# Keys of both inputs from one moving operand, and six modulation pieces one block earlier

## The chip, the cores and the metric

One core of one Trainium2 chip runs the whole kernel. The metric is the device time of one execution in microseconds. Its engines are named as in the profile: PE multiplies matrices, and PEld is its loading of weights (the stationary operand); DVE, ACT and POOL work on vectors; SP issues most transfers. One matmul step `X @ W` of this kernel keeps fp32 precision by splitting both operands into a high and a low part (`hi`, `lo`) and adding hi x hi, hi x lo and lo x hi.

## The reference, cut to what matters

x and ctx are 256 x 2048 each; the width of the attention is 1024 (16 heads of 64).

```python
hl = modulate(rms_norm(xl, norm1_g), mod_l[0], mod_l[1])      # x,   256 x 2048
hc = modulate(rms_norm(xc, norm1_g), mod_c[0], mod_c[1])      # ctx, 256 x 2048
zl = hl @ w_in + b_in                                         # conv | gMLP | q | k | v | gates
zkv = hc @ w_in[:, K_OFF:G_OFF] + b_in[K_OFF:G_OFF]           # ctx: keys and values alone
y_na = neighbourhood_attention(q, k, v, kc, vc, rpb)          # x attends to itself and to ctx
y = g_conv * conv_branch(zl) + g_sgu * sgu_branch(zl) + g_att * (y_na @ w_na_out)
xl = xl + mod_l[2] * (y @ w_o + b_o)
h2 = modulate(rms_norm(xl, norm2_g), mod_l[3], mod_l[4])
xl = xl + mod_l[5] * (square(relu(h2 @ w_ff1 + b_ff1)) @ w_ff2 + b_ff2)
out = rms_norm(xl, final_g)
```

The modulation vectors `mod_l`, `mod_c` are `silu(c) @ w_mod` for the two condition vectors.

## The kernel before, in words

All large weights come through one stream (`Stream`, L69). SP loads pieces of 512 KB into one of 8 `raw` buffers (L96); for a weight that is multiplied, ACT copies the high part (`whi`, L102) and DVE subtracts to get the low part (`wlo`, L105), each with 4 buffers. A list of steps is written by hand: each step names its pieces and a function that issues its work, and pieces are fetched up to 4 ahead (AHEAD).

*Stage 1, keys and values.* The 16 blocks of 128 along the width (`kt`) come in five blocks (BLOCKS, L34: 2, 2, 4, 4 and 4 of them). Each begins when its part of the first modulation is there (`mod_block`): `rows` (L393) transposes the normed inputs, and ACT and DVE write the scaled input and its low part into `hl` (high part in the first 256 of 512 columns, low part in the second). A heap unit of 4 KB a partition holds two kt of one input (L400 to L404). Then `kv_block` (L416) does the keys: `kfn` goes over tiles of 128 key columns (index i, nt) and both inputs v, with a PSUM bank for each (four banks `acc` in all). `mm_w` issues for each kt one matmul of 512 columns (`whi` by high and low part, L203) into the whole bank, then one of 256 (`wlo` by the high part, L205) into its second half. The two halves must be joined: ACT copies the second half (L438), DVE adds the first (L439), and POOL adds it to the keys so far, `kT` (L440); in block 0 ACT adds the bias (L435) and DVE joins (L436). Values (`vfn`, `mm_x`, L212 to L215) take the input as the stationary operand and the weights as the moving one, three matmuls of 512 columns per kt, and DVE adds the bank to `vN` (L456).

*Modulation pieces.* The other four modulation chunks are made by DVE alone: each piece (`mod_cols`, L932) brings two 128x512 row blocks of `w_mod` by SP, and DVE does two multiply-adds into `ga` (L944, L946). Every eighth piece ends with PE work (`col_finish`, transposes L975, or `row_finish`). `mod_steps(n)` puts n of them into the list; after each step of the last key and value block (bi 4) there are MODS_KV = 2, so 12 in all (L1026 to L1030).

*Stage 2* makes queries (`q_done`), convolution inputs (`a1_done`, `a2_done`, into `uT`), the gMLP halves (`gu`, `sv`), with the attention's steps between: `att_keys` (L538) writes the split keys into new units `kh`, `kl` and loads a bias tile (`bias_tile`, L563), `att_scores`, `att_transpose` and `att_out` follow, the last into `oT`. The 248 taps of the convolution are DVE instructions (`conv_taps`, L682 to L692), put between steps and reaching into stage 3; with the last tap `uT` goes out of use.

*Stage 3, the branches* (L1094 on), n = 0 attention, n = 1 gMLP, n = 2 convolution: for each of four column blocks cb, the gate's matmuls with x (`g_done`, L893, then a tanh) and the branch's output projection (`y_done`, L901), which for n = 0 writes into a new unit `mN[cb]`. Beside n = 0 the gMLP's norm and mixing run (`sgu_var`, L848: squares into a unit `svq`; `sgu_norm`, L861; `sgu_mix`, L865). All units come from one pool of HEAP = 27 (L57, `unit`, L183); a new one waits until the earlier user of its place is done.

Of the kernel before, what the change touches and what calls it, by code (L numbers as in the profile page):

```python
# [8 lines left out]
F32 = mybir.dt.float32  # L9
# [6 lines left out]
P = 128  # L16
# [15 lines left out]
GC1 = 0.7978845608028654  # L32

BLOCKS = [(0, 2), (2, 2), (4, 4), (8, 4), (12, 4)]  # L34
MODS_KV = 2
EARLY = 4
EARLY0 = 3
EARLYX = 2
# [125 lines left out]
def tile_block(ctx: ExitStack, tc: tile.TileContext, x, c, ctxt, c_ctx, w_mod, b_mod, norm1_g, norm2_g,  # L164
# [138 lines left out]

    m1A = cp.tile([P, NK, 2], F32, name="m1A")
    m1B = cp.tile([P, NK, 2], F32, name="m1B")
    hl = [[None] * NK, [None] * NK]
    kT = [None] * 8
    vN = [None] * 4

# [33 lines left out]
    def mod_block(bi):  # L343
        k0, nk = BLOCKS[bi]
        cols = nk * P
        rt = 1024 // cols
        gb = {}

        def mk(j, r0):
            def fn(raw):  # L350
                if r0 == 0:
                    gb[j] = aux("gemv")
                for r in range(rt):
                    g = r0 + r
                    q = g % 4
                    PE.matmul(gb[j][32 * q : 32 * q + 32, :cols], lhsT=cst[:, g], rhs=raw[:, r],
                              start=g < 4, stop=g >= NK - 4, tile_position=(0, 32 * q))
                if bi == 0 and (j, r0) != (1, NK - rt):
                    for r in range(rt):
                        q = (r0 + r) % 4  # L360
                        PE.matmul(warm()[32 * q : 32 * q + 32, :cols], lhsT=cst[:, r0 + r], rhs=raw[:, r],
                                  start=True, stop=True, tile_position=(0, 32 * q))
            return fn

        steps = []
        for j in range(2):
            for r0 in range(0, NK, rt):
                steps.append(([piece(w_mod, r0, rt, j * D + k0 * P, cols, False)], mk(j, r0)))

        def post(vs=(0, 1)):  # L370
            if vs[0] == 0:
                vectors()
            rows(vs)
            if bi == 0 and vs == (0,):
                for i in range(12):
                    PE.transpose(warm()[:, :P], gb["ge"][:, :P], ident)

        def vectors():
            gv = tp.tile([P, 2, 4, 2], F32, tag="gv", bufs=2, name=nm("gv"))
            for j in range(2):  # L380
                ge = tmp(512, "ge")
                S.copy(ge[:, :cols], gb[j][:, :cols])
                gp = aux("gp")
                for i in range(nk):
                    PE.transpose(gp[:, i * P : (i + 1) * P], ge[:, i * P : (i + 1) * P], ident)
                V.tensor_reduce(gv[:, j, :nk], gp[:, :cols].rearrange("p (i a b) -> p i b a", a=4, b=32)[:, :, :2], axis=AX.X, op=ALU.add)
            gb["ge"] = ge
            ks = slice(k0, k0 + nk)
            V.tensor_tensor(m1B[:, ks], gv[:, 0, :nk], both(bm0[:, ks]), ALU.add)
            V.tensor_tensor(m1A[:, ks], gv[:, 1, :nk], both(bm1[:, ks]), ALU.add)  # L390
            V.tensor_tensor(m1A[:, ks], m1A[:, ks], both(n1g[:, ks]), ALU.mult)

        def rows(vs):  # L393
            for v in vs:
                for kt in range(k0, k0 + nk):
                    scaled(v, kt // 4)
                    tps = aux("hT")
                    for t in range(2):
                        PE.transpose(tps[:, t * P : (t + 1) * P], nat[v][kt // 4][:, t, (kt % 4) * P : (kt % 4 + 1) * P], ident)
                    if kt % 2 == 0:  # L400
                        hl[v][kt] = unit([P, 2, 512], F32R, "h")
                    else:
                        hl[v][kt] = hl[v][kt - 1]
                    dst = hl[v][kt][:, kt % 2]  # L404
                    sA, sB = m1A[:, kt, v : v + 1], m1B[:, kt, v : v + 1]
                    last["hi"] = S.activation(dst[:, :T], tps[:, :T], AF.Identity, bias=sB, scale=sA)
                    f = tmp(256, "hf")
                    V.tensor_scalar(f, tps[:, :T], sA, sB, ALU.mult, ALU.add)
                    last["h"] = V.tensor_tensor(dst[:, T:], f, dst[:, :T].bitcast(F32), ALU.subtract)

        return steps, post

    def H(v, kt):
        return hl[v][kt][:, kt % 2]

    def kv_block(bi):  # L416
        k0, nk = BLOCKS[bi]
# [3 lines left out]
        def kfn(p, vs=(0, 1)):  # L421
            def fn(*ws):
                hi, lo = ws[0]
                n = kc // P if bi == 0 and p == 0 and vs == (0,) else 1
                for i0 in range(0, kc // P, n):
                    bs = {(i, v): bank("k") for i in range(i0, i0 + n) for v in vs}
                    mm_w([(b, hi, lo, j, i * P, H(v, k0 + j), j == 0, j == nk - 1) for (i, v), b in bs.items() for j in range(nk)])
                    for (i, v), b in bs.items():
                        nt = kc // P * p + i
                        if kT[nt] is None:  # L430
                            kT[nt] = kT[nt ^ 1] = unit([P, 2, 512], name="kT")
                        d = kT[nt][:, nt % 2, v * T : (v + 1) * T]
                        f = tmp()
                        if bi == 0:
                            S.activation(f, b[:, T:], AF.Identity, bias=par["k"][:, nt : nt + 1])  # L435
                            V.tensor_tensor(d, b[:, :T], f, ALU.add)  # L436
                        else:
                            S.copy(f, b[:, T:])  # L438
                            V.tensor_tensor(f, b[:, :T], f, ALU.add)  # L439
                            GP.tensor_tensor(d, d, f, ALU.add)  # L440
            return fn

        def vfn(cb, vs=(0, 1)):
# [74 lines left out]
    def q_done(p):  # L518
        def fn(i, b):
            nt = 2 * p + i  # L520
            f, g = tmp(), tmp()
            S.activation(f, b[:, T:], AF.Identity, bias=par["q8"][:, nt : nt + 1], scale=0.125)
            V.scalar_tensor_tensor(g.rearrange("p (r c) -> p r c", c=64)[:, :, ::-1],
                                   b[:, :T].rearrange("p (r c) -> p r c", c=64), 0.125,
                                   f.rearrange("p (r c) -> p r c", c=64), ALU.mult, ALU.add)
            if i == 0:
                qT[nt] = qT[nt + 1] = unit([P, 2, 2, T], F32R, "qT")
            q = qT[nt][:, i]
            up, dn = slice(0, 64), slice(64, P)
            S.copy(q[up, 0], g[up])  # L530
            S.copy(q[dn, 1], g[dn])
            V.tensor_tensor(q[dn, 0], g[up], q[up, 0].bitcast(F32), ALU.subtract)
            V.tensor_tensor(q[up, 1], g[dn], q[dn, 1].bitcast(F32), ALU.subtract)
        return fn
# [3 lines left out]
    def att_keys(nt):  # L538

        bias_tile(nt)  # L540
        k = kT[nt][:, nt % 2]
        hi = unit([P, 2, 512], F32R, "kh")
        lo = unit([P, 2, 512], F32R, "kl")
        kW[nt] = hi, lo
        half = [slice(0, 64), slice(64, P)]
        for r in range(2):
            S.copy(hi[half[r], r], k[half[r]])
            S.copy(hi[half[1 - r], r], k[half[r]])
        for r in range(2):
            V.tensor_tensor(lo[half[r], r], k[half[r]], hi[half[r], r].bitcast(F32), ALU.subtract)  # L550
        for r in range(2):
            S.copy(lo[half[1 - r], r], lo[half[r], r].bitcast(F32))

    mask = cp.tile([P, 64], F32, name="mask")
    GP.memset(mask, 0.0)
# [17 lines left out]
    def att_scores(h):  # L573
# [5 lines left out]
        for t in range(2):  # L579
            b = aux("S")  # L580
            hi, lo = kW[nt]
            q = qT[nt][:, nt % 2, h % 2, t * P : (t + 1) * P]
            PE.matmul(b, lhsT=q, rhs=hi[:, h % 2], start=True, stop=False)  # L583
            PE.matmul(b, lhsT=q, rhs=lo[:, h % 2], start=False, stop=True)  # L584
            V.tensor_tensor_reduce(s[:, t, :T], b[:, :T], bt[nt][:, h % 2, (2 - 2 * t) * 64 : (6 - 2 * t) * 64],
                                   scale=-1.0, scalar=BIG, op0=ALU.add, op1=ALU.min, accum_out=mx[:, 2 * t : 2 * t + 1])
            V.tensor_tensor_reduce(s[:, t, T:], b[:, T:], zero, scale=-1.0, scalar=mx[:, 2 * t : 2 * t + 1],
# [23 lines left out]
    def att_out(nt):  # L611
        b = aux("o")
        pts = [pT.pop(2 * nt), pT.pop(2 * nt + 1)]
        for kt in range(4):
            for j in range(2):
                h = 2 * nt + j
                PE.matmul(b[64 * j : 64 * j + 64, :T], lhsT=vN[kt][:, h * 64 : h * 64 + 64], rhs=pts[j][:, kt], start=kt == 0, stop=kt == 3)  # L617
        if nt % 2 == 0:
            oT[nt] = oT[nt + 1] = unit([P, 2, 512], F32R, "oT")
        o = oT[nt][:, nt % 2]  # L620
        bv = b[:, :T].rearrange("p (r c) -> p r c", c=64)[:, :, ::-1]
        S.copy(o[:, :T].rearrange("p (r c) -> p r c", c=64), bv)
        V.tensor_tensor(o[:, T:].rearrange("p (r c) -> p r c", c=64), bv,
# [395 lines left out]
    for bi in range(len(BLOCKS)):  # L1019
        kv = kv_block(bi)  # L1020
        for i, s in enumerate(kv):
# [4 lines left out]
            st.steps.append(s)  # L1026
            n = EARLY if bi else (EARLY0 if i == POS0 else EARLYX if i > POS0 else 0)
            st.steps += early[sent : sent + n]
            if bi == len(BLOCKS) - 1:
                mod_steps(MODS_KV)  # L1030
            sent += n
        if bi == 1:
# [49 lines left out]
    def xb_load(cb):  # L1082
        def fn():
# [7 lines left out]
            for t in range(2):  # L1091
                V.tensor_tensor(xb[cb][:, t], xb[cb][:, t], bo, ALU.add)
        return fn

    branches = [(2, w_na_out[0], lambda kt: oT[kt][:, kt % 2]), (1, w_sgu_out[0], lambda kt: sgT[kt][:, kt % 2]),
                (0, w_conv_out[0], lambda kt: cvT[kt][:, kt % 2])]
    for n, (br, w, xs) in enumerate(branches):
        for cb in range(4):
# [228 lines left out]
```

## Time and profile before

| | |
|---|---|
| median of 3 runs | 1750.83 us (1750.73 to 1752.44) |
| the profiled execution | 1752.01 us |
| its span, first to last instruction | 1750.2 us |
| PE busy | 1719.4 us (98%) |
| DVE busy | 1333.6 us (76%) |
| ACT busy | 874.6 us (50%) |
| POOL busy | 127.3 us (7%) |
| mean granted TensorE clock | 0.997 |

Busy times are of the whole span; a stage can have another fullest engine than the whole. Keys and values take 29.8 to 256.9 us, block 4 of them 207.3 to 256.9. In a timeline, successive matmuls overlap, so their pace is read from the start of one group to the start of the next; an idle time stands in brackets with what released the engine.

### The profile page before, as it was taken

The page shows a single profiled execution, that of the slowest core. Times are in us where ns is not written, and L with a number is a line of the kernel's source. Part 1 is how long each engine was busy: PE and PEld are TensorE (multiplying, and loading weights), DVE is VectorE, ACT ScalarE, POOL GpSimd, SP SyncE. Part 2 cuts the span into 40 slices and gives each one's busy share as a digit, 9 for nine tenths or more (in the row PEclk, how much of TensorE's full clock was granted, in tenths as well). Part 3 has the DMA queues.
Part 4 walks back from the last instruction along what each step waited for, and adds up shares of the span by engine and source line. Part 5 has one row for each costly group of instructions (what it writes and reads, how often), then busy time and mean ns, then how long its engine had stood idle before and what let it go on. Part 6 is the DMA issues. An engine that isn't in the chain of part 4 may idle for free.

```text
span 1750.2 us, 24238 instructions
## 1 busy us (share of the span) xinstructions
PE 1719.4 (98%) x8849; PEld 1426.7 (82%) x8849; DVE 1333.6 (76%) x2088; ACT 874.6 (50%) x1298; POOL 127.3 (7%) x179
## 2 busy tenths in 40 slices
PE   6999999999999999999999999999999999999997
PEld 4667878788888888788888888888888888888886
DVE  4655789799999987997889878756885576666665
ACT  4433427986545444564444565434543455335543
POOL 2222230110000010200000010000000000000000
PEclk9999999999999999999999999999999999999999
DMA  9898578657667778898898977867886776666552
GB/s 322 283 322 272 151 221 255 185 141 214 198 191 225 226 235 279 271 314 297 291 300 296 316 238 251 259 194 225 276 270 195 220 241 191 204 193 190 187 195 79
DMA packets 266969, 411.87 MB, mean 235 GB/s; under 512 B 13182, under 2 KB 128050, under 8 KB 266850
## 3 DMA queue, kind: packets, MB, share of 16 engines
q1 hardware_dynamic: 259410, 391.21, 68.9%
q0 software_dynamic: 6864, 18.07, 4.4%
q8 instruction: 69, 1.13, 0.3%
q10 hardware_dynamic: 576, 1.05, 0.2%
q14 instruction: 50, 0.41, 0.1%
HBM read 408.18 MB, written 2.10 MB: 234 GB/s over the span
## 4 chain that ended last, share of the span: by engine, by line
PE 79%; DVE 1%; ACT 1%; issue 0%; POOL 0%; POOLq 0%; DVEq 0%
PE bk L203 18%; PE bk L212 16%; PE bk L213 16%; PE bk L215 16%; PE bk L205 9%; PE o L617 1%; PE pT L606 1%; PE S L584 0%; PE S L583 0%; DVE wlo L105 0%; PE mrow L965 0%; PE mix L871 0%; PE mT L920 0%; ACT whi L102 0%; PE x1T L1138 0%
## 5 line engine op out<-in xcount | busy, mean ns | idle before, releaser
L102 ACT CAST whi<-raw 128x1024 fp32r<-128x1024 f32 x544 | 571.3, 1052 | 663.8 <-PE bk L213 430.3
L105 DVE TENSOR_TENSOR wlo<-raw,whi 128x1024 fp32r<-128x1024 f32 x544 | 670.3, 1234 | 285.2 <-ACT whi L102 274.9
L203 PE MATMUL bk<-h,whi 128*128 128x512 f32 x1536 | 395.1, 394 | 0.2 <-DVE h L1190 0.2
L203 PEld LDWEIGHTS bk<-h,whi 128*128 128x128 f32 x1536 | 273.8, 189 | 50.7 <-issue 2.7
L205 PEld LDWEIGHTS bk<-h,wlo 128*128 128x128 f32 x1536 | 216.0, 190 | 19.4
L205 PE MATMUL bk<-h,wlo 128*128 128x256 f32 x1536 | 221.7, 282 | 0.0
L213 PE MATMUL bk<-whi,g 128*128 128x512 f32 (+1 forms) x516 | 199.7, 387 | 0.0
L212 PE MATMUL bk<-whi,g 128*128 128x512 f32 (+1 forms) x516 | 199.7, 387 | 0.0
L946 DVE SCALAR_TENSOR_TENSOR ga<-raw,cst,ga 128x512 f32<-128x512 f32 x240 | 186.4, 777 | 2.1
L212 PE MATMUL bk<-whi,h 128*128 128x512 f32 x448 | 175.4, 392 | 0.0
L213 PE MATMUL bk<-whi,h 128*128 128x512 f32 x448 | 174.4, 389 | 0.0
L215 PE MATMUL bk<-wlo,g 128*128 128x512 f32 (+1 forms) x516 | 139.3, 387 | 0.0
L215 PE MATMUL bk<-wlo,h 128*128 128x512 f32 x448 | 122.2, 389 | 0.0
L212 PEld LDWEIGHTS bk<-whi,g 128*128 128x128 f32 x516 | 96.9, 188 | 19.7
L213 PEld LDWEIGHTS bk<-whi,g 128*128 128x128 f32 x516 | 96.9, 188 | 19.7
L215 PEld LDWEIGHTS bk<-wlo,g 128*128 128x128 f32 x516 | 96.5, 188 | 19.8
L692 DVE SCALAR_TENSOR_TENSOR cT<-uT,wcT,cT 128x249 f32<-128x249 f32 (+14 forms) x240 | 103.6, 476 | 0.6
L215 PEld LDWEIGHTS bk<-wlo,h 128*128 128x128 f32 x448 | 84.1, 188 | 17.5
L213 PEld LDWEIGHTS bk<-whi,h 128*128 128x128 f32 x448 | 84.1, 188 | 17.1
L212 PEld LDWEIGHTS bk<-whi,h 128*128 128x128 f32 x448 | 84.1, 188 | 17.0
L203 PE MATMUL k<-h,whi 128*128 128x512 f32 x256 | 69.2, 404 | 4.9 <-DVE t L439 2.5
L440 POOL TENSOR_TENSOR kT<-kT,t 128x256 f32<-128x256 f32 x64 | 52.6, 845 | 139.8 <-DVE t L439 139.5
(276 smaller groups left out, 1975.5 us busy)
## 6 DMA issues: line engine op xcount, KB each, us to landing
raw<-in_w_ff_dram SPq DMA_DIRECT2D x256, 512.0 KB, 4.4
raw<-in_w_in_dram SPq DMA_DIRECT2D x208, 512.0 KB, 4.7
raw<-in_w_mod_dram SPq DMA_DIRECT2D x192, 512.0 KB, 5.4
raw<-in_w_o_dram SPq DMA_DIRECT2D x32, 512.0 KB, 5.5
raw<-in_w_na_out_dram SPq DMA_DIRECT2D x16, 512.0 KB, 4.5
raw<-in_w_sgu_out_dram SPq DMA_DIRECT2D x16, 512.0 KB, 5.6
raw<-in_w_conv_out_dram SPq DMA_DIRECT2D x16, 512.0 KB, 5.4
bias<-in_na_rpb_dram POOLq DMA_DIRECT2D x16, 192.0 KB, 4.9
```

Source lines behind the costliest of these rows:

```text
L102: nc.scalar.copy(hv, rv)
L105: self.low[j] = nc.vector.tensor_tensor(lv, rv, hv.bitcast(F32), ALU.subtract)
L203: PE.matmul(bk, lhsT=hi[:, j, c0 : c0 + P], rhs=xhl, start=start, stop=False)
L205: PE.matmul(bk[:, T:], lhsT=lo[:, j, c0 : c0 + P], rhs=xhl[:, :T], start=False, stop=stop)
L212: PE.matmul(bk, lhsT=xhl[:, t * P : (t + 1) * P], rhs=hi, start=start, stop=False)
L213: PE.matmul(bk, lhsT=xhl[:, T + t * P : T + (t + 1) * P], rhs=hi, start=False, stop=False)
L215: last["mm"] = PE.matmul(bk, lhsT=xhl[:, t * P : (t + 1) * P], rhs=lo, start=False, stop=stop)
L440: GP.tensor_tensor(d, d, f, ALU.add)
L606: PE.transpose(b[:, kt * T + t * P : kt * T + (t + 1) * P], s[:, t, (2 * g + kt) * P : (2 * g + kt + 1) * P], ident)
L617: PE.matmul(b[64 * j : 64 * j + 64, :T], lhsT=vN[kt][:, h * 64 : h * 64 + 64], rhs=pts[j][:, kt], start=kt == 0, stop=kt == 3)
L692: V.scalar_tensor_tensor(a[:, lo:hi], u[:, lo + d : hi + d], wj, a[:, lo:hi], ALU.mult, ALU.add)
L946: V.scalar_tensor_tensor(a[0], raw[:, r], sc, a[0], ALU.mult, ALU.add)
```

## The change

MODS_KV is 1, and the modulation steps follow every step of blocks 3 and 4 instead of block 4 alone: six pieces in each. A unit of `hl` now holds both inputs of one kt (16 units instead of 8 and 8). For blocks 1 to 4, `mm_both` gives PE the high parts of both inputs as one moving operand of 512 columns, in two segments of 256, then both low parts, then the high parts by `wlo`: three matmuls of 512 columns for each kt into one bank, and one DVE add of 128x512 into `kT`. Block 0 has three matmuls of 256 columns for each kt and input (`mm_one`), and ACT alone writes `kT`. The context's half of a unit (`spare_half`) serves after the keys and values: `qT` and later `oT` in units 0 to 7, the split keys in units 8 to 15, so these take no units of their own.

```diff
-MODS_KV = 2
+MODS_KV = 1
...
-    hl = [[None] * NK, [None] * NK]
+    hl = [None] * NK
...
-                    if kt % 2 == 0:
-                        hl[v][kt] = unit([P, 2, 512], F32R, "h")
-                    else:
-                        hl[v][kt] = hl[v][kt - 1]
-                    dst = hl[v][kt][:, kt % 2]
+                    if hl[kt] is None:
+                        hl[kt] = unit([P, 2, 512], F32R, "h")
+                    dst = hl[kt][:, v]
...
     def H(v, kt):
-        return hl[v][kt][:, kt % 2]
+        return hl[kt][:, v]
+
+    def spare_half(kt):
+
+        return hl[kt][:, 1]
+
+    def mm_both(b, hi, lo, c0, kts):
+
+        bv = b.rearrange("p (v t) -> p v t", v=2)
+        for j, kt in enumerate(kts):
+            PE.matmul(bv, lhsT=hi[:, j, c0 : c0 + P], rhs=hl[kt][:, :, :T], start=j == 0, stop=False)
+            PE.matmul(bv, lhsT=hi[:, j, c0 : c0 + P], rhs=hl[kt][:, :, T:], start=False, stop=False)
+        for j, kt in enumerate(kts):
+            PE.matmul(bv, lhsT=lo[:, j, c0 : c0 + P], rhs=hl[kt][:, :, :T], start=False, stop=j == len(kts) - 1)
+
+    def mm_one(todo):
+
+        for bk, hi, lo, j, c0, xhl, start, stop in todo:
+            PE.matmul(bk[:, :T], lhsT=hi[:, j, c0 : c0 + P], rhs=xhl[:, :T], start=start, stop=False)
+            PE.matmul(bk[:, :T], lhsT=hi[:, j, c0 : c0 + P], rhs=xhl[:, T:], start=False, stop=False)
+        for bk, hi, lo, j, c0, xhl, start, stop in todo:
+            PE.matmul(bk[:, :T], lhsT=lo[:, j, c0 : c0 + P], rhs=xhl[:, :T], start=False, stop=stop)
...
+                if bi:
+                    for i in range(kc // P):
+                        nt = kc // P * p + i
+                        b = bank("k")
+                        mm_both(b, hi, lo, i * P, range(k0, k0 + nk))
+                        d = kT[nt][:, nt % 2]
+                        V.tensor_tensor(d, d, b, ALU.add)
+                    return
...
-                        d = kT[nt][:, nt % 2, v * T : (v + 1) * T]
-                        f = tmp()
-                        if bi == 0:
-                            S.activation(f, b[:, T:], AF.Identity, bias=par["k"][:, nt : nt + 1])
-                            V.tensor_tensor(d, b[:, :T], f, ALU.add)
-                        else:
-                            S.copy(f, b[:, T:])
-                            V.tensor_tensor(f, b[:, :T], f, ALU.add)
-                            GP.tensor_tensor(d, d, f, ALU.add)
+                        S.activation(kT[nt][:, nt % 2, v * T : (v + 1) * T], b[:, :T], AF.Identity, bias=par["k"][:, nt : nt + 1])
...
-            if i == 0:
-                qT[nt] = qT[nt + 1] = unit([P, 2, 2, T], F32R, "qT")
-            q = qT[nt][:, i]
+            q = qT[nt] = spare_half(nt).rearrange("p (h t) -> p h t", h=2)
...
-        hi = unit([P, 2, 512], F32R, "kh")
-        lo = unit([P, 2, 512], F32R, "kl")
+        at = 8 + 4 * (nt % 2)
+        hi = [spare_half(at + r) for r in range(2)]
+        lo = [spare_half(at + 2 + r) for r in range(2)]
...
-        if nt % 2 == 0:
-            oT[nt] = oT[nt + 1] = unit([P, 2, 512], F32R, "oT")
-        o = oT[nt][:, nt % 2]
+        o = oT[nt] = spare_half(nt)
...
-            if bi == len(BLOCKS) - 1:
+            if bi > 2:
                 mod_steps(MODS_KV)
```

## Rows read from the trace of the kernel before

**Rows 1.** The page's table of engines: busy us (share of the span) xinstructions.

```profile
PE 1719.4 (98%) x8849; PEld 1426.7 (82%) x8849; DVE 1333.6 (76%) x2088; ACT 874.6 (50%) x1298; POOL 127.3 (7%) x179
```

**Rows 2.** Timeline of PE, 217 to 235: start, length, operation, count [idle <-releaser].

```profile
223.38 2.11 PE L203 MATMUL k<-h,whi 128*128 128x512 f32 x8 [1.71 <-DVE t L439]
...
230.00 2.11 PE L203 MATMUL k<-h,whi 128*128 128x512 f32 x8 [0.76 <-DVE t L439]
...
234.74 0.44 PE L975 MATMUL mcol<-ident,ga 128*128 128x128 f32 x2 [1.45 <-DVE ga L946]
```

**Rows 3.** Waits, 205 to 245: engine, line, releaser: us, times, longest.

```profile
PEld k L203 <- DVE t L439: 3.1, 3, 1.9
...
PEld mcol L975 <- DVE ga L946: 1.8, 1, 1.8
```

**Rows 4.** Groups of DVE, 207 to 257 (block 4): count | busy us, mean ns.

```profile
L946 DVE SCALAR_TENSOR_TENSOR ga<-raw,cst,ga 128x512 f32<-128x512 f32 x22 | 20.6, 938 | 0.2
...
L439 DVE TENSOR_TENSOR t<-k,t 128x256 f32<-128x256 f32 x16 | 6.0, 413 | 0.4 <-ACT t L438 0.4
```

**Rows 5.** Timeline of PE: a key cycle of block 3, a value cycle of block 2.

```profile
171.28 2.00 PE L203 MATMUL k<-h,whi 128*128 128x512 f32 x8
173.12 1.12 PE L205 MATMUL k<-h,wlo 128*128 128x256 f32 x8
174.07 2.00 PE L203 MATMUL k<-h,whi 128*128 128x512 f32 x8
...
133.85 1.07 PE L215 MATMUL vb<-wlo,h 128*128 128x512 f32 x4
...
136.57 1.07 PE L215 MATMUL vb<-wlo,h 128*128 128x512 f32 x4
```

**Rows 6.** A window of block 3: us; busy PE, PEld, DVE, ACT, POOL; clock, DMA, GB/s.

```profile
180.00:190.00 10.00, 10.00 (x50) 8.40 (x49) 3.96 (x7) 1.88 (x4) 6.55 (x9) 1.00 0.41 120
```

**Rows 7.** Groups of DVE, 542.4 to 637.5, with columns as in rows 4.

```profile
L105 DVE TENSOR_TENSOR wlo<-raw,whi 128x1024 fp32r<-128x1024 f32 x34 | 41.9, 1234 | 0.0
L692 DVE SCALAR_TENSOR_TENSOR cT<-uT,wcT,cT 128x245 f32<-128x245 f32 (+13 forms) x67 | 30.9, 495 | 0.2
L946 DVE SCALAR_TENSOR_TENSOR ga<-raw,cst,ga 128x512 f32<-128x512 f32 x10 | 7.9, 793 | 0.0
L907 DVE SCALAR_TENSOR_TENSOR m<-th,bk 128x512 f32<-128x512 f32 x6 | 4.1, 681 | 0.0
L897 DVE TENSOR_TENSOR th<-bk,gb 128x512 f32<-128x512 f32 x6 | 4.0, 683 | 0.0
L873 DVE TENSOR_TENSOR t<-mix,bs 128x128 f32<-128x128 f32 x16 | 3.9, 284 | 0.0
L874 DVE TENSOR_TENSOR t<-t,gu 128x256 f32<-128x256 f32 x8 | 3.4, 421 | 0.0
L759 DVE SCALAR_TENSOR_TENSOR sg<-t,sg 128x256 fp32r<-128x256 f32 x8 | 3.4, 421 | 0.0
L862 DVE SCALAR_TENSOR_TENSOR sv<-sv,sgu_var,lg 128x1024 f32<-128x1024 f32 x2 | 2.6, 1282 | 0.6 <-POOL sgu_var L859 0.6
L863 DVE TENSOR_TENSOR sv<-sv,lb 128x1024 f32<-128x1024 f32 x2 | 2.4, 1218 | 0.0
```

**Rows 8.** The taps' line, 500 to 640: ns min/median/max, first and last start.

```profile
L692 DVE SCALAR_TENSOR_TENSOR cT<-uT,wcT,cT x110: 458/476/955, 499.8 to 637.0; 128x246 f32<-128x246 f32 x8, 128x247 f32<-128x247 f32 x8, 128x248 f32<-128x248 f32 x8, 128x249 f32<-128x249 f32 x8
```

**Rows 9.** Timeline of PE behind y of column block 1.

```profile
597.83 0.60 PE L871 MATMUL mix<-ws,sv 128*128 128x128 f32 x4
```

**Rows 10.** The squares' line on ACT, columns as in rows 8.

```profile
L856 ACT ACTIVATE svq<-sv x2: 1045/1052/1058, 542.5 to 543.6; 128x1024 f32<-128x1024 f32 x2
```

**Rows 11.** Timeline of PE at the first keys, and a window behind it (columns: rows 6).

```profile
29.85 1.05 PE L203 MATMUL k<-h,whi 128*128 128x512 f32 x3 [1.95 <-ACT whi L102]
...
30.00:34.00 4.00, 4.00 (x14) 3.34 (x15) 3.44 (x4) 1.90 (x5) 0.00 (x0) 0.57 1.05 385
```

**Rows 12.** The page's DMA issues: issue, count, KB each, us to landing.

```profile
bias<-in_na_rpb_dram POOLq DMA_DIRECT2D x16, 192.0 KB, 4.9
```

More of the change, by code (lines that the diff above doesn't have):

```diff
@@ L423, in fn @@
                 hi, lo = ws[0]
-                n = kc // P if bi == 0 and p == 0 and vs == (0,) else 1
+                if bi:
[6 more added lines that the diff above has]
+                    return
+                n = kc // P if p == 0 and vs == (0,) else 1
                 for i0 in range(0, kc // P, n):
                     bs = {(i, v): bank("k") for i in range(i0, i0 + n) for v in vs}
-                    mm_w([(b, hi, lo, j, i * P, H(v, k0 + j), j == 0, j == nk - 1) for (i, v), b in bs.items() for j in range(nk)])
+                    mm_one([(b, hi, lo, j, i * P, H(v, k0 + j), j == 0, j == nk - 1) for (i, v), b in bs.items() for j in range(nk)])
                     for (i, v), b in bs.items():
@@ L546, in att_keys @@
         for r in range(2):
-            S.copy(hi[half[r], r], k[half[r]])
-            S.copy(hi[half[1 - r], r], k[half[r]])
+            S.copy(hi[r][half[r]], k[half[r]])
+            S.copy(hi[r][half[1 - r]], k[half[r]])
         for r in range(2):
-            V.tensor_tensor(lo[half[r], r], k[half[r]], hi[half[r], r].bitcast(F32), ALU.subtract)
+            V.tensor_tensor(lo[r][half[r]], k[half[r]], hi[r][half[r]].bitcast(F32), ALU.subtract)
         for r in range(2):
-            S.copy(lo[half[1 - r], r], lo[half[r], r].bitcast(F32))
+            S.copy(lo[r][half[1 - r]], lo[r][half[r]].bitcast(F32))
     mask = cp.tile([P, 64], F32, name="mask")
@@ L581, in att_scores @@
             hi, lo = kW[nt]
-            q = qT[nt][:, nt % 2, h % 2, t * P : (t + 1) * P]
-            PE.matmul(b, lhsT=q, rhs=hi[:, h % 2], start=True, stop=False)
-            PE.matmul(b, lhsT=q, rhs=lo[:, h % 2], start=False, stop=True)
+            q = qT[nt][:, h % 2, t * P : (t + 1) * P]
+            PE.matmul(b, lhsT=q, rhs=hi[h % 2], start=True, stop=False)
+            PE.matmul(b, lhsT=q, rhs=lo[h % 2], start=False, stop=True)
             V.tensor_tensor_reduce(s[:, t, :T], b[:, :T], bt[nt][:, h % 2, (2 - 2 * t) * 64 : (6 - 2 * t) * 64],
@@ L1093, in xb_load @@
         return fn
-    branches = [(2, w_na_out[0], lambda kt: oT[kt][:, kt % 2]), (1, w_sgu_out[0], lambda kt: sgT[kt][:, kt % 2]),
+    branches = [(2, w_na_out[0], lambda kt: oT[kt]), (1, w_sgu_out[0], lambda kt: sgT[kt][:, kt % 2]),
                 (0, w_conv_out[0], lambda kt: cvT[kt][:, kt % 2])]
```

## The prediction

> **What bounds the kernel now.** I read the page's table of engines first: PE is busy 1719.4 of 1750.2 us [rows 1], so a gain comes only from PE's few idle gaps or from shorter PE work, and any new gap costs its full length. Hence I looked for the gaps. In the timeline of PE in key and value block 4, key cycles start at 223.38 and 230.00 after 1.71 and 0.76 us idle, and the modulation's transposes at 234.74 after 1.45 us [rows 2]. The waits of that stretch name what came last: DVE's join of the keys (L439) and DVE's modulation product (L946) [rows 3]. So there DVE, not PE, sets the pace. The groups of DVE in block 4 [rows 4] say with what: 20.6 us of modulation (L946) and 6.0 us of joins, beside the splits. Per piece of key weights (four k, two key tiles of 128 columns) it is a split of 1.23 us [rows 7], the two products of each of two modulation pieces, 4 x 0.94, and four joins of 0.41: 6.6 us, where PE needs two cycles of 2.79, 5.6 us (a cycle runs from 171.28 to 174.07 [rows 5]). In block 3 DVE has room: 3.96 of 10.00 us are busy in 180 to 190, with the DMA engines at 0.41 [rows 6]. The third view is the DVE table of 542.4 to 637.5, the branch stage, where DVE is the fullest engine although PE shows no gap [rows 7].
>
> **The change, part by part.**
>
> *Stalls of block 4.* The six pieces moved to block 3 take 12 x 0.94 = 11.3 us of DVE and six 512 KB loads on SP's queue with them. They are paid in block 3 out of the 6 us in 10 that rows 6 show idle; SP's loads there go past key and value pieces in a stretch with the DMA engines under half busy, so I cost them at nothing (if that cover were gone, a block 3 step would wait a landing, below 5 us). In blocks 3 and 4 alike DVE's work per key piece is then 1.23 + 2 x 0.94 + two adds of 128x512, priced as the adds of L897 at 0.68 [rows 7], = 4.5 us, below PE's 5.4, so the gaps close and none opens in block 3. Their size: by PE's gaps 1.71 + 0.76 + 1.45 = 3.9 [rows 2], by the waits of its weight loads 3.1 + 1.8 = 4.9 [rows 3]; I take 4.5, ends 3.0 (if the transposes' wait on L946 stays) and 4.9.
>
> *PE's matmuls, blocks 1 to 4.* Now eight 512-column and eight 256-column matmuls for four k and both inputs take 2.79 us; after, twelve of 512. The nearest row is a value cycle, twelve of 512, 133.85 to 136.57 = 2.72 [rows 5]: 0.07 us less for each of 24 such cycles in blocks 2 to 4, and half as much for 8 in block 1: 28 x 0.07 = 2.0 us. No row shows a moving operand in two segments 2 KB apart. Its bounds: no dearer than the value cycle's (-2.0), or each 512 as dear as two of 256 ((174.07 - 173.12)/8 = 0.119 us each, [rows 5]): 12 x 0.238 = 2.85 us, +0.06 x 28 = +1.7. I take -2.0, since the count of columns per matmul is that of the value cycle.
>
> *Block 0.* Per k and input three of 256 (0.36 us) replace one of 512 and one of 256 (0.23 + 0.12 = 0.35): 32 x 0.01 = +0.3. Bounds: 0 to +0.5.
>
> *Joins, copies, POOL adds.* They run on DVE, ACT and POOL beside PE; outside block 4 they cost nothing now, as PE shows no gap there, so their removal gives nothing more.
>
> *Slots.* The pool of 4 KB units has 27 (HEAP, line 57). Before, a unit holds one input's `hl` of two k; eight carry x through the gates, the context's eight go free after block 4. After, all 16 units live until the last gate; queries, split keys and outputs move into their spare halves. Counted from the code at the start of the attention branch's gates: before 8 (h) + 4 (oT) + 2 cT + 1 uT + 2 gu + 2 sv + 4 (ws, lg, lb, bs) = 23. After 16 + 2 + 1 + 2 + 2 + 4 = 27: full. Yet `svq` (L854) and then `mN[0]` (L906) want a slot, which before they found. The first to come free is uT[1], with the last convolution tap, which in this trace starts at 637.0 [rows 8]; y_done (L907) for column block 0 cannot write before that. What is queued: two of PE's four banks stay held by y of block 0; PE can still do gates and y of block 1 in the other two, whose y ends where the mix at 597.83 begins [rows 9], less the three mixes of 0.6 us at most that came before it and now don't, so about 596.4. Behind `svq` wait the norms (L862, L863), the mixes and sgT.
>
> When do the taps end then? DVE no longer does before them what hangs on the slots or on PE past 596.4, by the counts and means of rows 7: y_done 4.1, mixes 3.9 + 3.4 + 3.4, norms 2.6 + 2.4, two of six L897 1.3, some 12 of 34 splits 14.9, four of ten L946 3.2; together 39.2 us. The ten rows sum to 104.5 us in 95.1 us elapsed (neighbours overlap), so 39.2 x 0.91 = 35.7 us: the taps end at about 637.5 - 35.7 = 601.8. Then two Squares into `svq` of 1.05 us on ACT [rows 10] with their accumulator reads, some 2.5, one after the other, and one y_done, 0.7: PE goes on at 605.0, a gap of 8.6 us. Bounds: 0, if the slot comes free before PE needs it (the shortage removes no PE work, so no gain), and 13, if only 9 splits and two products fall out (33.9 x 0.91 = 30.8, taps until 606.7). PE gets slower after a gap: after 1.95 us idle at 29.85 the granted clock of 30 to 34 is 0.57, the lower of the two levels (1.2 and 2.4 GHz) for most of it [rows 11], so (1 - 0.57) x 4 = 1.7 us. Together +10.3, bounds 0 and +15.
>
> *Attention.* The pool is fuller by up to three units when the queries begin, which can delay a bias tile; its load lands 4.9 us after issue [rows 12]. Bounds 0 and +4.9; I take +0.5, as the spare halves take back what qT, kh, kl and oT used.
>
> **Sum:** -4.5 - 2.0 + 0.3 + 10.3 + 0.5 = +4.6 us. The profiled execution took 1752.0, 1.2 over the median 1750.83 of the runs shown; on the median that gives 1755.4, put as 1755.5. A measurement of this kernel can tell about 0.2% (3.5 us) from no change: below 1747.3 is faster, above 1754.3 slower.
>
> **The rivals.**
>
> *The slots don't bite (not slower).* The order of allocation may give `mN[0]` or `svq` a place in time: one unit freed earlier than I count (a bias tile, gu, a released h) is enough, or taps that DVE takes ahead of splits. Deciding point: the last tap before about 593. For it: the count rests on lifetimes read from the code, and a miscount of one or two suffices. Against it: the 16 units of `hl` are certain, as the gates read the x half of each. Time: 1750.8 - 6.2 + 0.5 = 1745.1, faster.
>
> *The keys' matmuls pay for the stride (slower still).* With the two-segment operand at the upper bound, +1.7 in place of -2.0, the sum is +8.3: 1759.1. Place: the key steps of blocks 1 to 4; it decides nothing on the sign alone, since the gap's 10.3 does, but would add to it. For it: nothing in this trace reads PE's moving operand so. Against it: columns, not segments, separate 0.23 from 0.12 in rows 5.
>
> A rule speaks against the gain in matmuls as well. By rows 5 a 512 takes (173.12 - 171.28)/8 = 0.230 us from start to start and a 256 0.119, so two of each 0.698, and three of a value cycle 0.68. The Trainium skill, page "TensorE: Matmul & The Clock Gate", section "Back-to-back issue gap", gives columns/2.4 + 2.5 ns for an isolated stream: by it an estimated 0.650 against 0.647 us, nothing gained, and the sum would be +6.6. The trace's 0.119 for 256 columns doesn't agree with its 0.109, so the sum goes by the rows. As a rival this is "no gain in PE's stream": -2.0 becomes 0, 1757.5.
>
> **How the numbers follow.** Slots bite as costed 0.56, its own range 1751 to 1760 (gap 4 to 13 us), of it a little over half above 1754.3; slots don't bite 0.31; stride or no gain in the stream together 0.13, with the slots biting. Faster: nearly all of 0.31 and a little of 0.56, 0.32. Slower: 0.6 of 0.56 and most of 0.13, 0.43. Within: 0.25. The range takes in both sides, as each holds more than 2 in 10: from 1743.5 (stalls 4.9, no attention cost) to 1760.5.
>
> **What would show it.** In the profile after: no idle before key steps and `mcol` in block 4; L439, L440 gone and key cycles of 2.72 us; block 3 still without PE gaps; 3 to 13 us of PE idle around 590 to 600, released by DVE's y_done, with the last tap and then L856 just ahead of it, and a granted clock near the lower level behind it. Wrong: no gap there, or L856 before the taps end (the second case); key cycles of 2.85 us (the third); idle before the value steps of block 3; or PE waiting for bias tiles in 290 to 400.

## The result, and the profile after

The changed kernel took 1761.80 us (median; 1760.82 to 1762.39) against 1750.78 for the kernel before: ratio 1.0061, interval 1.0049 to 1.0073, so slower by about 11 us. That is the forecast sign, but 1.3 us above the top of the range. The profiled executions' spans, 1760.6 and 1750.2, differ by 10.4 us, which the trace has to account for.

From the first query on, PE issues the same large matmuls in both kernels, so the start of the same matmul can be compared. Of those that write a bank `bk` I took the first, the 193rd and so on, and subtracted the start in the trace before; a change from column to column is time won or lost between. The table has the experiments too. e9 is the kernel before with one unit more in the pool and nothing of the change, so its line shows how far two traces can differ without it:

```
start before, us   257.5   296.6   550.2   602.1   750.0   950.1  1700.0
after              -5.95   -7.42   -1.14   +8.97   +9.10  +10.31  +10.36
e1 mods only       -3.73   -4.42   -4.41   -4.40   -4.39   -4.40   -4.34
e2 keys only       -5.62   -7.07   -1.86   +7.13   +7.29   +9.33   +9.35
e3 stage 3 freed   -6.34   -7.78   -3.23   -3.23   -3.19   -1.72   -1.66
e4 28 units        -6.26   -7.71   -8.21   -8.20   -8.21   -7.97   -7.90
e5 e2 + POOL adds  -0.88   -2.32   +1.96  +11.87  +11.99  +13.63  +13.66
e6 before, 4 held  -0.21   -0.61   -0.61   +8.21   +8.33   +8.36   +8.42
e9 before, 28 un.  -0.82   -1.22   -0.94   -0.94   -0.91   -0.87   -0.80
```

Read the second line: keys and values won 5.95 us, the attention stage gave back 4.8 net (-5.95 to -1.14), the branch stage lost 10.1 around 600 us, and 1.4 went later. Not all of the 5.95 is the change's: the trace before has the lower clock at the first keys [rows 11], e9's has not (below). Against e9's line the same steps are 5.1 won, then 4.9, 10.1 and 1.3 lost, in all +11.2, close to the 11.0 between the medians. The page's table of engines, against [rows 1], shows none of this, since PE's busy time hardly moves:

```profile
PE 1720.3 (98%) x8769; PEld 1422.0 (81%) x8769; DVE 1313.7 (75%) x2040; ACT 853.4 (48%) x1234; POOL 76.7 (4%) x115
```

**Keys and values.** The timeline of PE in block 4 after the change: key cycles follow each other every 2.72 us, and the modulation's transposes (now L991) start with no idle time in brackets, where [rows 2] had gaps before them:

```profile
208.64 1.07 PE L425 MATMUL k<-h,wlo 128*128 128x512 f32 x4
...
211.36 1.07 PE L425 MATMUL k<-h,wlo 128*128 128x512 f32 x4
...
217.71 0.60 PE L991 MATMUL mcol<-ident,ga 128*128 128x128 f32 x4
```

By the starts of their first matmuls, blocks 1 to 3 take 63.13 to 207.29 before and 61.69 to 206.83 after, so 1.0 us longer, with two new idle times of PE, 0.31 and 0.60 us. Block 4, to the first query, takes 50.2 before and 44.7 after. Block 1 began 1.4 us earlier after. Most of that is not the change: at the first keys the granted clock of 30 to 34 is 0.57 before, after 1.95 us idle, but 1.00 in e9, whose keys are the same and whose PE was idle 1.75 us there, and block 1 begins at 62.24 in e9.

**Attention.** The waits from 285 to 400 us (engine, line, releaser: us, times, longest). The copy that begins a bias tile now waits for the scores' reading of an earlier tile (L603); the scores wait for the tile's landing; the o matmuls wait for the scores (L605):

```profile
POOL bias L585 <- DVE mx L603: 72.1, 5, 17.1
...
PE o L635 <- DVE mx L605: 5.0, 5, 1.4
DVE s L603 <- DMA bias<-in_na_rpb_dram: 4.4, 2, 2.8
```

The timeline shows the circle for one pair of heads. POOL copies the mask at 358.84, right behind the last reading L603 at 358.35; the load's second half lands at 365.27, and the next pair's scores start at 365.44:

```profile
358.35 0.42 DVE L603 CUSTOM_DVE_ANT_0 s<-S,bias 128x256 f32<-128x256 f32 x1
...
358.84 0.83 POOL L585 COPY bias<-mask 128x768 f32<-128x768 f32 x1 [17.14 <-DVE mx L603]
359.96 2.04 POOL L589 DMA_DIRECT2D bias<-in_na_rpb_dram  x2 [0.30 <-POOL bias L585]
365.44 0.42 DVE L603 CUSTOM_DVE_ANT_0 s<-S,bias 128x256 f32<-128x256 f32 x1 [1.64 <-DMA bias<-in_na_rpb_dram]
```

The same holds for pairs 2, 4, 6 and 7; pair 3 starts 1.1 us after its landing. From the trace, when the tile had landed and when its first scores began:

```
pair of heads            2       3       4       5       6       7
before: landed       303.13  325.80  336.57  365.52  378.52  396.86
        scores       319.24  333.50  351.98  367.28  384.31  403.54
after:  landed       314.56  327.63  347.76  365.27  384.00  402.10
        scores       314.72  328.77  347.92  365.44  384.17  402.26
```

One releaser misleads here. The DVE timeline puts the wait at 384.17 down to a PE matmul; but that wait ends 0.17 us after the tile landed, like those of the other pairs. The S matmul it needs had started 3.9 us earlier.

```profile
384.17 0.43 DVE L603 CUSTOM_DVE_ANT_0 s<-S,bias 128x256 f32<-128x256 f32 x1 [3.15 <-PE bk L205]
```

The o matmuls' five waits are 5.0 us of the stage's loss. The size differs from trace to trace: in e2, e3 and e5, which run the same attention code, these waits sum to 4.1, 3.4 and 3.2 us, and the table's loss from the first column to the third is 3.8, 3.1 and 2.8, against 4.8 here. PE also waits 1.99 us at 302.59 for the modulation's products (L991 for DVE's L962); e4 has that wait too (1.63), so it is not the tiles'.

**Branch stage.** The timeline around 600 us, against [rows 8 to 10]. The last taps end at 598.86, the first square starts 0.04 us later, the second follows the first, then y_done (now L923), and 0.8 us after y_done's start PE goes on, after 6.51 us:

```profile
597.89 0.97 DVE L708 SCALAR_TENSOR_TENSOR cT<-uT,wcT,cT 128x242 f32<-128x242 f32 x2
...
598.90 1.06 ACT L872 ACTIVATE svq<-sv 128x1024 f32<-128x1024 f32 x1 [2.62 <-DVE cT L708]
...
600.08 1.06 ACT L872 ACTIVATE svq<-sv 128x1024 f32<-128x1024 f32 x1
...
601.34 1.27 DVE L923 SCALAR_TENSOR_TENSOR m<-th,bk 128x512 f32<-128x512 f32 x2
...
602.16 0.76 PE L212 MATMUL bk<-whi,h 128*128 128x512 f32 x1 [6.51 <-DVE m L923]
```

The window behind it has the clock in the seventh place after the length, as in [rows 11]: 0.50, the lower level, for six microseconds:

```profile
602.00:608.00 6.00, 5.84 (x16) 4.81 (x17) 5.28 (x6) 1.04 (x1) 0.82 (x2) 0.50 0.16 44
```

### The profile page after: what moved, and what is told of

The parts are those of the page before. It is cut to its first block, busy times and chain, and to the rows that moved or that the text cites. A ratio compares the mean times of both kernels' runs of the same rounds, so it can differ in the third digit from the quotient of the medians.

```text
span 1760.6 us, 23816 instructions
## 1 busy us (share of the span) xinstructions
PE 1720.3 (98%) x8769; PEld 1422.0 (81%) x8769; DVE 1313.7 (75%) x2040; ACT 853.4 (48%) x1234; POOL 76.7 (4%) x115
## 4 chain that ended last, share of the span: by engine, by line
PE 91%; DVE 4%; DMA 2%; ACT 1%; issue 1%; SPq 0%; POOL 0%; POOLq 0%; DVEq 0%; ACTq 0%
PE bk L203 19%; PE bk L212 16%; PE bk L213 16%; PE bk L215 16%; PE bk L205 9%; PE gemv L356 2%; PE k L422 2%; PE k L423 1%; DVE wlo L105 1%; PE vb L215 1%; PE k L425 1%; PE vb L212 1%; PE vb L213 1%; DMA raw<-in_w_in_dram 1%; PE o L635 1%
## 5 line engine op out<-in xcount | busy, mean ns | idle before, releaser
L212 PE MATMUL bk<-whi,h 128*128 128x512 f32 x512 | 201.6, 394 | 6.6 <-DVE m L923 6.5
L213 PE MATMUL bk<-whi,h 128*128 128x512 f32 x512 | 200.4, 391 | 0.0
L962 DVE SCALAR_TENSOR_TENSOR ga<-raw,cst,ga 128x512 f32<-128x512 f32 x240 | 182.2, 759 | 2.2
L215 PE MATMUL bk<-wlo,h 128*128 128x512 f32 x512 | 140.9, 391 | 0.0
L212 PEld LDWEIGHTS bk<-whi,h 128*128 128x128 f32 x512 | 96.6, 189 | 27.4 <-ACT svq L872 6.9
L215 PEld LDWEIGHTS bk<-wlo,h 128*128 128x128 f32 x512 | 96.5, 189 | 20.2
L213 PEld LDWEIGHTS bk<-whi,h 128*128 128x128 f32 x512 | 96.7, 189 | 19.7
L708 DVE SCALAR_TENSOR_TENSOR cT<-uT,wcT,cT 128x244 f32<-128x244 f32 (+14 forms) x240 | 101.9, 467 | 0.6
L212 PE MATMUL vb<-whi,h 128*128 128x512 f32 x128 | 51.1, 401 | 0.3 <-ACT whi L102 0.3
L212 PE MATMUL bk<-whi,mhl 128*128 128x512 f32 (+1 forms) x132 | 50.9, 388 | 0.0
```

The source lines that it names most:

```text
L212: PE.matmul(bk, lhsT=xhl[:, t * P : (t + 1) * P], rhs=hi, start=start, stop=False)
L213: PE.matmul(bk, lhsT=xhl[:, T + t * P : T + (t + 1) * P], rhs=hi, start=False, stop=False)
L215: last["mm"] = PE.matmul(bk, lhsT=xhl[:, t * P : (t + 1) * P], rhs=lo, start=False, stop=stop)
L708: V.scalar_tensor_tensor(a[:, lo:hi], u[:, lo + d : hi + d], wj, a[:, lo:hi], ALU.mult, ALU.add)
L962: V.scalar_tensor_tensor(a[0], raw[:, r], sc, a[0], ALU.mult, ALU.add)
```

## The experiments

### Which half of the change wins the keys' time

e1 is the kernel before with the modulation's part of the change alone:

```diff
-MODS_KV = 2
+MODS_KV = 1
...
-            if bi == len(BLOCKS) - 1:
+            if bi > 2:
```

> The kernel before with the six modulation pieces moved to block 3 and nothing else. Theory (the key steps of block 4 wait for DVE, whose surplus is the modulation): the gaps of block 4 close, block 3 stays without one, 3 to 5 us less than before, near 1746.3. Rival (the joins of the keys are the surplus, and any second load on DVE does as well): the gaps stay or move into block 3, within 1 us of before.

Measured: ratio 0.9987 (0.9978 to 0.9996), 2.3 us by the medians, less than the 3 to 5 expected, and 4.3 by the spans; its runs spread from 1747.0 to 1751.5, and the reason for that stays open. PE's timeline in block 4 has one gap left, where [rows 2] had three:

```profile
222.66 2.11 PE L203 MATMUL k<-h,whi 128*128 128x512 f32 x8 [0.41 <-DVE t L439]
```

Block 3 took the six pieces nearly without a gap (0.22 and 0.06 us of PE idle, and 0.7 us longer from its first key matmul to block 4's), though DVE is now 9.24 us of 10 busy in the window of [rows 6], against 3.96:

```profile
180.00:190.00 10.00, 10.00 (x48) 8.31 (x48) 9.24 (x12) 1.97 (x4) 6.70 (x9) 1.00 0.87 276
```

e2 is the changed kernel with that edit undone, so the keys' part alone:

> The changed kernel with all twelve modulation pieces back in block 4. Theory: DVE needs 1.23 + 3.76 + 1.36 = 6.4 us per key piece against 5.44 of PE, so about half of block 4's gaps come back: 1 to 4 us more than the changed kernel, 1763 to 1766. Rival (the join alone was the cause): no gap in block 4, 1761.8. The gap near 600 and the late bias tiles stay in both.

Measured: 1761.41 us, 0.4 below the changed kernel, and no gap in block 4. The theory fell. From its first key matmul to the first query, block 4 takes 50.2 us before, 46.1 in e1, 44.8 in e2 and 44.7 after. The sum had the product L946 at 0.94 us; without POOL's adds the same operation (now L962) takes 0.75, so DVE needs 1.22 + 4 x 0.746 + 2 x 0.68 = 5.6 us per key piece, hardly more than PE's 5.44. The groups of DVE, 206.8 to 229, in e2 (beside [rows 4]):

```profile
L962 DVE SCALAR_TENSOR_TENSOR ga<-raw,cst,ga 128x512 f32<-128x512 f32 x13 | 9.7, 746 | 0.1
L105 DVE TENSOR_TENSOR wlo<-raw,whi 128x1024 fp32r<-128x1024 f32 x5 | 6.1, 1222 | 1.4 <-ACT whi L102 1.4
```

e5 puts POOL's adds back into e2, without any use:

```diff
                         V.tensor_tensor(d, d, b, ALU.add)
+                        for _ in range(2):
+                            GP.tensor_tensor(tmp(256, "gd"), d[:, :T], d[:, T:], ALU.add)
                     return
```

> The kernel of e2 with two 128x256 adds on POOL behind each key tile of blocks 1 to 4, into a scratch tile that nobody reads, as many as before. Theory (POOL's adds slow DVE's operations on two fp32 tiles: L946 took 1.05 us with them and 0.75 without, splits 1.33 and 1.22): the modulation products of block 4 come back to 0.95 to 1.05 us, DVE needs over 5.44 us per key piece again and PE gaps return in block 4, 1 to 4 us more than e2. Rival (they were slow for another reason, such as loads landing or the joins' order): 0.75 us stays, e2's time within 1 us.

Measured: 1766.47, 5.1 us over e2, a little beyond the expected end; block 4 takes 49.7. The product is at 0.91 us again and the split at 1.48 (groups of DVE, 206.8 to 229):

```profile
L964 DVE SCALAR_TENSOR_TENSOR ga<-raw,cst,ga 128x512 f32<-128x512 f32 x12 | 11.0, 914 | 0.1
L105 DVE TENSOR_TENSOR wlo<-raw,whi 128x1024 fp32r<-128x1024 f32 x4 | 5.9, 1479 | 0.5 <-ACT whi L102 0.5
```

And a gap of 3.44 us before the transposes returns (timeline of PE):

```profile
232.24 1.11 PE L993 MATMUL mcol<-ident,ga 128*128 128x128 f32 x4 [3.44 <-DVE ga L964]
```

So the gaps of block 4 had a third cause beside modulation and joins: POOL's adds stretch DVE's operations on two tiles in SBUF. The add into `kT` (L449), which reads one operand from PSUM, does not change: 0.680 us in e2, 0.675 in e5. The size for the kernel before is not shown by e5, as its adds on POOL take 1.26 us each and those before 0.96. The Trainium skill, page "SBUF — State Buffer", section "SBUF: two separate sides", says that a DVE operation with two inputs in SBUF and a GpSimd operation that reads SBUF take one shared pair of ports in turn, each for its whole length. These traces agree in that the DVE operation takes longer, 0.75 us without and 0.91 to 0.94 with them; that they go in turn is not shown here.

### What the full pool costs

e3 takes the squares and sgT out of the pool in the branch stage and lets bs in only behind the norms; the cT, uT, gu, sv, ws, lg and lb units stay:

```diff
-        sq = unit([P, 1024], name="svq")
-        S.activation(sq, sv[t], AF.Square, accum_out=sg["v"][:, t : t + 1])
+        for r in range(2):
+            S.activation(spare_half(12 + 2 * t + r), sv[t][:, 512 * r : 512 * r + 512], AF.Square, accum_out=sg["vv"][:, t, r : r + 1])
...
+        if t == 1:
+            sg["bs"] = unit([P, 8, P], name="bs")
+            GP.dma_start(sg["bs"], bcast(sgu_b[0], P))
...
-            sgT[g] = sgT[g + 1] = unit([P, 2, 512], F32R, "sg")
+        sgT[g] = spare_half(8 + g)
```

> The changed kernel with three users taken out of the pool in the branch stage: the squares go to spare halves, the mixes' result sgT too, and bs is loaded behind the norms. Theory (a full pool makes mN[0] wait for uT[1], and so for the last tap): the 6.5 us gap and the low clock behind it go, about 10 us less than the changed kernel, 1750 to 1753; the attention stage stays as it is. Rival (DVE is simply behind there, as its taps, splits and modulation fill it): PE still waits for DVE near 600, less than 3 us gained.

Measured: 1751.46 us, 10.3 below the changed kernel. The window shows PE busy throughout where the gap was, with DVE just as full, which rules the rival out:

```profile
590.00:612.00 22.00, 22.00 (x105) 18.42 (x104) 22.00 (x44) 8.78 (x12) 0.00 (x0) 1.00 0.71 231
```

e6 asks the opposite: the kernel before, layout and keys untouched, with four units held through that stage. The edit releases them with the last gate of the convolution branch (`br` 0; its adds run at 934.6 to 935.2 us), so later than the expectation says, and as late as the changed kernel's 16 units of `hl`.

```diff
+    held4 = []
+    def hold():
+        for _ in range(4):
+            d_ = unit([P, 1024], name="held")
+            GP.memset(d_[:, :8], 0.0)
+            held4.append(d_)
...
+    st.do(hold)
     st.do(sv_init)
     st.do(sgu_load)
```

> The kernel before with four units of the pool held from the gMLP's value half to the last gate of the attention branch, as the contexts' halves hold them after; keys, layout and attention stay. Theory (the full pool alone makes the gap): a PE gap of 4 to 9 us near 597, released by y_done behind the squares behind the last tap, and a low clock behind it, 8 to 12 us over before, 1759 to 1763. Rival (the gap needs the new layout): no gap, before's time.

Measured: 1761.11 us, 10.2 over before; its profiled execution has +8.8 of that between the third and the fourth column of the table. Its timeline has the same gap to the hundredth:

```profile
602.66 0.76 PE L212 MATMUL bk<-whi,h 128*128 128x512 f32 x1 [6.51 <-DVE m L919]
```

e4 is the changed kernel with one unit more. Its room comes from `ah`, 4 KB of the temporaries that are not used before 700 us and now share other buffers:

```diff
-HEAP = 27
+HEAP = 28
...
-            ah = tp.tile([P, 2, 512], F32R, tag="ah", bufs=1, name=nm("ah"))
+            ah = [tp.tile([P, 512], F32R, tag="tmp512", bufs=7, name=nm("ah")) for _ in range(2)]
```

> The changed kernel with one more unit in the pool, 28 (the split modulation row ah takes its room from the temporaries). Theory: a bias tile can be loaded one pair of heads earlier, so the scores no longer wait for its landing, 3 to 5 us less in the attention stage; in the branch stage mN[0] finds the one unit and mN[1] does not, so the gap comes a column block later or goes, 4 to 10 us less: together 1747 to 1755. Rival for the attention stage (the keys and queries in spare halves tie ACT, DVE and PE to each other, whatever the pool): the o matmuls still wait about 1 us per pair of heads, and only the branch stage gains.

Measured: 1744.74 us, ratio to before 0.9963 (0.9950 to 0.9975): 17.1 us under the changed kernel, a little more gain than expected, since the one unit ends both losses altogether. In the table the column of 550 us has -8.21 where the changed kernel has -1.14, and the next shows no step. The copy for pair 5 starts at 351.38 instead of 358.84 and no o matmul waits for scores, though the scores of pairs 5 and 6 still start 0.16 us after their tile lands. The window from 290 to 400 of e3, which still has the late tiles, has 104.30 us of PE (columns as in [rows 6]):

```profile
290.00:400.00 110.00, 104.30 (x642) 87.86 (x641) 93.55 (x238) 94.41 (x181) 16.78 (x18) 1.00 0.59 158
```

That of e4 has 108.37:

```profile
290.00:400.00 110.00, 108.37 (x672) 91.35 (x671) 99.48 (x256) 98.00 (x189) 16.94 (x18) 1.00 0.63 167
```

The rival for the attention stage falls: keys and queries lie in spare halves in both.

Four more runs close the account. e7 has 29 units and one raw buffer less:

> The kernel of e4 with 29 units and one raw buffer less (7). Theory: with 28 the pool no longer holds PE up anywhere, so a further unit gives nothing and the buffer costs nothing: within 1 us of e4, 1744 to 1746. Rival (the scores still wait for some bias tiles): 1 to 2 us less than e4.

1746.38 us: 1.6 over e4, a miss, on the other side from the rival. Its starts lie 0.6 us behind e4's at the first query, 0.2 at 900 us and 1.3 from 940 on; whether the buffer alone costs that was not tried. e8 joins e3 and e4:

> e3 and e4 together: 28 units, and squares, sgT and bs out of the pool's way in the branch stage. Theory: the gap is gone in e4 already, so nothing is left to gain: 1744 to 1746. Rival: a wait for slots is left further down the branch stage, up to 2 us less than e4.

1744.38, as e4. e9 gives the kernel before the 28 units, by e4's edit:

> The kernel before with the pool of e4, 28 units. Theory (only the change filled the pool): the kernel before has no wait for a unit that PE feels, so within 1 us of before, 1750 to 1752. Rival (a 28th unit helps whatever the layout, so e4's gain is not the change's): 2 us or more less than before.

1751.19, ratio 1.0001 (0.9992 to 1.0010): nothing, so e4's gain is that of the change. e10 is e2 with 28 units:

> The kernel of e4 with all twelve modulation pieces in block 4: e2 with 28 units. Theory (without POOL's adds DVE keeps up in block 4, so the move of the six pieces adds nothing): within 1 us of e4, 1744 to 1746. Rival (the move carries a share of the gain once the pool no longer hides it): 1.5 to 4 us over e4, 1746 to 1749.

1744.27, as e4: with the keys from one operand, the move of the six pieces is worth nothing that can be measured.

## Why the prediction was right and wrong

- **Stalls of block 4, -4.5:** three gaps of 3.9 went, as [rows 2] gave them, and block 4 is 5.5 us shorter. But the working named the wrong pieces: modulation alone shortens the block by 4.1 (e1), the keys alone by 5.4 (e2), both by 5.5. They are two cures for one surplus, and the prediction priced L946 at 0.94 on both sides, not seeing that POOL's adds made it so. That no gap opens in block 3 holds nearly: of the 0.60 us idle there e2, without the six pieces, has 0.57.
- **PE's matmuls, -2.0:** right for the matmuls. A key cycle takes 2.72 us, the value cycle's time, so neither the two segments 2 KB apart nor the rule that nothing is gained bore out. As time it came in block 4 alone: blocks 1 to 3, with 20 of the 28 cycles, are 1.0 us longer than before, of which 0.9 are the two new idle times; where the rest of the gain went stays open. That 5.95 us before the first query lies so near the sum's 6.2 is luck: 1.4 of it came before block 1, where e9, without the change, is 0.9 ahead of the trace before as well.
- **Slots, +10.3:** right in place, chain and nearly in size. By steps: last tap 598.9 for 601.8, squares 2.3 for 2.5, gap 6.5 for 8.6, clock 0.50 x 6.0 = 3.0 for 1.7; together 9.5 of the 10.1 in the table. That the total came so near is in part luck, as a shorter gap and a longer time at the lower clock make up for each other. The rival that the slots don't bite fell (e3, e6).
- **Attention, +0.5 with +4.9 as its end: the step that failed.** It read the cost as one tile that lands once too late, and let the spare halves pay for the rest. The pool stays as full through the whole stage, so every pair's tile could be ordered only when an earlier one had been read, and its landing of some 5 us stood before the scores of nearly each pair. Net 4.8 us, 4.3 over the value taken; with it the sum would have been +8.9. That 4.8 lies at the stated end is luck: the end stood for one whole landing, and the cost is five waits of 0.66 to 1.43 us.
- **Not in the sum:** 1.0 us between 935 and 940 of the trace before, at transposes of m (0.82 us in one idle time). Of the kernels with the new layout those with 28 units (e4, e8, e10) don't have it, but e7 with 29 and one raw buffer less does, so what makes it stays open. So does 1.5 us won between 257 and 297, which all kernels with the new keys show; part of it may be a gap of 0.85 us at 295 that the kernel before has and they don't.
- **The range:** its lower end, 1743.5, is a little below what its own terms give (1750.8 - 4.9 - 2.0 + 0.3 = 1744.2).

## What to carry to other kernels

When a change keeps a buffer alive longer, count the pool at every stage that allocates from it, not at one, and ask what waits behind each new unit. A wait that recurs with every head costs as often as the loop runs, so bound it by the loop, not by one occurrence. A full pool can hide a real gain: the same edit was 11 us slower at 27 units and 6.4 us faster at 28. And before a stall is put down to an engine's amount of work, look whether its instructions run at their usual price there: in the prediction's own rows the product L946 stands at 0.94 us in block 4 [rows 4] and at 0.79 in the branch stage [rows 7], and that was the sign of POOL's part.

## What the runs showed of the hardware that was not expected

POOL's 128x256 adds lengthened DVE's two-operand work in SBUF by a fifth (0.75 to 0.91 us; splits 1.22 to 1.48) and cost PE 4.7 us through DVE (e5 against e2, first column of the table).

The lower clock behind an idle time was not the same from trace to trace. After the same idle time of 6.51 us the window behind it has 0.50 for six microseconds in the changed kernel, about 3.0 us lost, but in e6 0.51 for three, about 1.5 lost, and 1.00 from there on:

```profile
602.70:605.70 3.00, 3.00 (x7) 2.41 (x8) 3.00 (x4) 0.00 (x0) 0.61 (x2) 0.51 0.23 67
```

At the first keys, 1.95 us idle before them, the trace before lost 1.7 us [rows 11]; in e6, after 2.05 us idle at the same place, the granted clock of 30 to 34 is 1.00, and the first eight matmuls take 2.09 us against 3.19. So the price that the prediction took for the clock was that of one trace.
